# Paired heads in layer B, and a joined, re-laid-out gate and up projection in the experts, of a three-block Trainium2 kernel

## The chip, the core and the metric

The kernel runs on one core of one Trainium2 chip. Its five engines have their own instruction lists: TensorE (PE, matmuls; PEld is its weight load), VectorE (DVE), ScalarE (ACT), GpSimd (POOL) and SyncE (SP, which here only issues DMAs). The metric is device time in microseconds of one execution, lower is better. A change is given against the median of the runs of the kernel before.

## The reference

Three residual blocks work on 512 tokens of 1024 channels, one sequence. The first two are a mixer and a mixture of 16 experts each: block 0 has a dilated attention (layer A here), block 1 the attention with forget gates (layer B). The third is a state-space and pooling block, which the change does not touch. What the change concerns:

```python
def forgetting_mixer(h, w_in, f_bias, w_out, q_gain, k_gain):        # the mixer of layer B
    """logit[t,s] = q_t.k_s/sqrt(d) + sum_{s<j<=t} log sigmoid(w_f.x_j + b_f), causal."""
    ...
    cum = jnp.cumsum(log_f, axis=1).transpose(0, 2, 1)
    q = rmsnorm(qkv[:, :, 0], q_gain) * ATTN_SCALE                   # 16 heads of 64
    k = rmsnorm(qkv[:, :, 1], k_gain)
    ...
    def block(args):                                                 # blocks of 128 queries
        i, q_i, c_i = args
        logits = jnp.einsum('bqhd,bkhd->bhqk', q_i, k).astype(jnp.float32)
        logits = logits + (c_i[..., None] - cum[:, :, None, :])
        mask = key_pos[None, :] <= q_pos[:, None]
        p = jax.nn.softmax(jnp.where(mask, logits, NEG_INF), axis=-1)
        return jnp.einsum('bhqk,bkhd->bqhd', p, v)
    ...
    return o.reshape(b, s, B_WIDTH).astype(h.dtype) @ w_out

def hierarchical_moe(h, wg_r, bg_r, we_r, be_r, w_gate, w_up, w_down):
    """Top-1 expert group, then top-2 experts inside it; SwiGLU experts, weighted by the gate."""
    ...
    gates = (g_onehot[:, :, None] * in_group[:, None, :]).reshape(-1, N_EXPERTS)
    hid = jax.nn.silu(jnp.einsum('nd,edf->nef', t, w_gate)) * jnp.einsum('nd,edf->nef', t, w_up)
    y = jnp.einsum('nef,efd->nd', hid * gates[..., None].astype(hid.dtype), w_down)
    return y.reshape(b, s, d)
```

An expert has a hidden width of 256, so its gate and up weights are 1024 x 256 each, its down weights 256 x 1024.

## The kernel before

One program does everything in sequence: layer A's mixer (0 to some 675 us), its output projection and routing (to 722), the experts of layer 1 (to 922), layer B's start (to 1000), its attention (to 1240), output projection and routing (to 1296), the experts of layer 2 (to 1505), block 2.

*Precision.* A product of two fp32 operands is made of three matmuls over fp32r halves: high times high, high times low, low times high. `split3` (L150, the matmul at L153) issues them. Splitting a weight tile takes an ACT copy to the high half (L315) and a DVE subtraction for the low half (L316). Some operands are left whole ("plain") and go in one fp32 matmul.

*Layer B's attention.* `mix_b` weaves two streams. The background stream is the projection of q, k and v of the head pair that comes later, 24 times three matmuls of 384 columns a pair. The foreground tasks are generators for each head pair: `forget_rows_of` makes normed and transposed q and k (two heads of 64 channels lie on the two halves of the 128 partitions), and `attn_forget`, once for each of the two heads, runs the query blocks 0 to 3. A block's scores have 128, 256, 384 or 512 columns; three matmuls over 64 rows make them in one of three PSUM score tiles (`sc`), and a fourth, of bf16 constants over 128 rows (L1385), adds the causal mask of the diagonal block. `softmax_piece` then takes the bias and the running bound on DVE (L473) and the exponential with its sum on ACT (L474); DVE normalises. `attn_values` transposes the probabilities, splits them, and multiplies by v. `weave` sets the order in which instructions are written: each task yields an estimate of its cost and a delay after which it is due (the numbers in the table `DL`, `bs` and `bp` among them); whichever is due goes in between projections. On PE this order is kept.

*The experts.* Weights are streamed from DRAM by SP. `expert_loads` issues six tiles of 512 KB an expert: gate in two halves, up in two halves, down in two. A tile of gate or up holds four chunks of 128 rows; partition p gets row p of each chunk, so a contiguous piece is one row of 256 numbers, 1 KB. There are 7 staging buffers `est`, 2 of `esp` and 4 extra; `expert_split` frees one when the split is done, and `load(n)` alternates a split and the next load. `token_list` turns an expert's routing ranks into a list of up to 96 tokens (four matmuls of one-hot columns, L949), from which POOL gathers the token rows `xg` from DRAM (`hd`, the normed rows) by an indirect DMA; four more matmuls make the gates (L957). `expert_in` transposes the gathered rows; for the first expert it gives a plain `xTf`, copied by ACT (L1010). `expert_half` runs 24 matmuls of 256 columns over the 8 chunks, once for gate and once for up. `expert_hidden`, `expert_out` and the scatter follow.

*Start of an expert stage.* Routing counts the tokens of each expert. If one has more than 96, an overflow loop has to run; `overflow` reads that flag into a register on every engine, and every engine compares and branches (L1070, L1071). Written order before: list 0, counts, gates, two loads, list 1, two loads, the transposes of the first expert's tokens, the overflow branch, two loads, list 2, loads, gates of experts 0 to 2, then the experts one by one. The data of this case never takes the overflow path.

*Normed rows.* `mix_end` writes the normed rows of each 128 tokens to DRAM after the last scaling (L1194, four a layer).

## Time and profile before

| what | value |
|---|---|
| median of 3 runs | 1851.56 us (1849.99 to 1854.08) |
| profiled execution | 1848.67 us, span of its instructions 1846.8 us |
| mean granted TensorE clock | 0.954 |
| busy, PE / PEld | 1665.7 us (90%) / 1469.2 us (80%) |
| busy, DVE / ACT / POOL | 1282.6 us (69%) / 926.5 us (50%) / 121.0 us (7%) |
| DMA over the whole span | 294141 packets, 310.83 MB, mean 168 GB/s |
| layer B's attention, 1000 to 1240 us | PE 233.55 us, DMA engines 0.20 busy |
| experts of layer 1, 722 to 922 us | PE 174.04 us, DMA engines 0.87 busy, 262 GB/s |
| experts of layer 2, 1296 to 1505 us | PE 173.25 us, DMA engines 0.85 busy, 256 GB/s |

The span runs from the first to the last instruction; the execution's own time is 1.9 us longer. A busy share over the whole span is an average over stages with different limits, so it is read stage by stage. In a timeline, the bracket behind a row is how long the engine had been idle and what ended that. "PEq" is PE's own sequencer: a time in which PE neither computes nor waits for another engine. In the rows, `x8` is eight instructions put together, and the start is that of the first.

### The profile page before, as it was taken

What the parts mean: (1) busy time and instruction counts of PE and PEld (TensorE: products, weight loads), DVE (VectorE), ACT (ScalarE), POOL (GpSimd) and SP (SyncE); (2) the same over time, 40 slices, a digit from 0 to 9 for tenths busy, and PEclk for the clock granted to TensorE, in tenths of its full rate; (3) what the DMA queues carried; (4) which work ended last, traced back from release to release, by engine and by line L of the source; (5) the groups of instructions that cost most, each with busy time, mean ns of one, the idle gap of its engine ahead of it and who ended that gap; (6) DMA issues with size and microseconds to landing.
All of it is one profiled execution on the core that took longest, in us unless ns stands there. A gap on an engine that the chain in (4) does not pass through costs nothing. (4 is left out here: it accounts for less than half of the span.)

```text
span 1846.8 us, 30370 instructions
## 1 busy us (share of the span) xinstructions
PE 1665.7 (90%) x11022; PEld 1469.2 (80%) x11023; DVE 1282.6 (69%) x3181; ACT 926.5 (50%) x1978; POOL 121.0 (7%) x95
## 2 busy tenths in 40 slices
PE   5979999999999996999869999999598959999998
PEld 3878998989989985787658798888487748788886
DVE  6748777767686657787656667666687755998574
ACT  4536556555565643566444555552465533454443
POOL 1000000000000001133200000000133210000000
PEclk9989999999999997999988899899799979999999
DMA  8886655556564136899753221126699953333331
GB/s 291 244 276 183 189 159 176 164 154 195 153 184 132 58 113 211 270 316 302 208 148 93 58 69 58 63 70 212 197 315 313 295 154 110 98 105 88 112 118 76
DMA packets 294141, 310.83 MB, mean 168 GB/s; under 512 B 31263, under 2 KB 240779, under 8 KB 293980
## 3 DMA queue, kind: packets, MB, share of 16 engines
...
## 5 line engine op out<-in xcount | busy, mean ns | idle before, releaser
L153 PE MATMUL mm<-whi,hThi 128*128 128x384 f32 (+2 forms) x1128 | 403.3, 358 | 5.4 <-ACT hThi L739 2.0
L153 PE MATMUL mm<-whi,hTlo 128*128 128x384 f32 (+2 forms) x1128 | 384.3, 341 | 1.0 <-DVE hTlo L740 0.5
L153 PE MATMUL mm<-wlo,hThi 128*128 128x384 f32 (+2 forms) x1128 | 382.6, 339 | 0.0
L316 DVE TENSOR_TENSOR wlo<-wst,whi 128x768 fp32r<-128x768 f32 (+2 forms) x200 | 200.1, 1011 | 67.5 <-ACT whi L315 65.0
L153 PEld LDWEIGHTS mm<-whi,hThi 128*128 128x128 f32 x1128 | 215.6, 191 | 13.9 <-ACT hThi L739 3.2
L315 ACT ACTIVATE whi<-wst 128x768 fp32r<-128x768 f32 (+2 forms) x200 | 176.6, 892 | 87.6 <-PE mm L153 54.2
L153 PEld LDWEIGHTS mm<-whi,hTlo 128*128 128x128 f32 x1128 | 214.9, 191 | 6.2 <-DVE hTlo L740 3.3
L316 DVE TENSOR_TENSOR ehl<-est,ehl 128x1024 fp32r<-128x1024 f32 x144 | 175.8, 1222 | 60.8 <-ACT ehl L315 60.1
L153 PEld LDWEIGHTS mm<-wlo,hThi 128*128 128x128 f32 x1128 | 216.0, 191 | 1.9 <-issue 0.6
L315 ACT ACTIVATE ehl<-est 128x1024 fp32r<-128x1024 f32 x144 | 152.1, 1058 | 105.0 <-PE sc L153 23.3
L153 PE MATMUL mm<-ehl,xTh 128*96 128x256 f32 x960 | 178.4, 287 | 0.0
L248 DVE SCALAR_TENSOR_TENSOR adacc<-ast,csil,adacc 128x512 f32<-128x512 f32 x168 | 126.1, 751 | 64.9 <-DMA ast<-in_w_ada_dram 62.9
L153 PE MATMUL mm<-ehl,xTl 128*96 128x256 f32 x480 | 136.0, 283 | 0.0
L153 PEld LDWEIGHTS mm<-ehl,xTh 128*96 128x96 f32 x960 | 134.7, 165 | 0.0
L153 PE MATMUL mm<-hThi,whi 128*128 128x512 f32 (+1 forms) x288 | 107.2, 372 | 0.7 <-ACT sza L1887 0.6
L153 PE MATMUL mm<-hTlo,whi 128*128 128x512 f32 (+1 forms) x288 | 106.0, 368 | 0.5 <-DVE hTlo L310 0.3
L153 PE MATMUL mm<-hThi,wlo 128*128 128x512 f32 (+1 forms) x288 | 105.8, 367 | 0.0
L415 ACT ACTIVATE raw<-mm 128x256 f32<-128x256 f32 x126 | 48.2, 382 | 110.2 <-PE mm L153 109.8
L420 DVE TENSOR_REDUCE qss<-sq 128x4 f32<-128x256 f32 x128 | 53.0, 414 | 63.3 <-ACT sq L417 63.1
L153 PEld LDWEIGHTS mm<-ehl,xTl 128*96 128x96 f32 x480 | 79.0, 165 | 0.0
L1226 POOL MEMSET xg<- 96x1024 f32 x6 | 5.5, 952 | 1066.5 <-PE sc L153 1066.5
L966 POOL DMA_INDIRECT xd<-y,tidx x32 | 66.6, 2083 | 112.8 <-DVE hTl L1048 87.4
...
## 6 DMA issues: line engine op xcount, KB each, us to landing
ast<-in_w_ada_dram SPq DMA_DIRECT2D x192, 256.0 KB
...
```

The source lines that it names most:

```text
L153: self.nc.tensor.matmul(out, lhsT=l, rhs=r, start=n_first and i == 0, stop=n_last and i == nt - 1)
L248: last = nc.vector.scalar_tensor_tensor(acc, st, self.csil[:, k:k + 1], acc, op0=ALU.mult, op1=ALU.add)
L315: nc.scalar.activation(hi, st, AF.Copy)
L316: nc.vector.tensor_sub(lo, st, hi.bitcast(F32))
L415: nc.scalar.activation(raw[:, t].rearrange("p a b -> p (a b)"), p[:, :256], AF.Copy)
L420: nc.vector.tensor_reduce(ss[:, 4 * t:4 * t + 4], sq.rearrange("p (g d) -> p g d", d=HD), axis=AX.X, op=ALU.add)
L966: self.nc.gpsimd.indirect_dma_start(out=dst, out_offset=bass.IndirectOffsetOnAxis(ap=idx, axis=0), in_=src, in_offset=None, bounds_check=S ...
L1226: nc.gpsimd.memset(xg, 0.0)
```

## The change

It has three parts.

*Layer B.* `attn_forget` is split in two. `forget_scores` takes both heads of a pair at once, in three groups: blocks 0 and 1 together in one score tile a head, then block 2, then block 3. Within a group the matmuls of the two heads alternate; the mask is added by two matmuls of 64 rows a head (`idh`, `maskh`, loaded by four small DMAs of POOL when the layer starts). `forget_values` does the values of both heads, as a task of its own when the scores are done. The planner's delays become `bs` 1.5 and `bp` 3.0, and a probability tile has two buffers.

*Experts.* A staging tile now holds gate and up of two chunks: two DMAs of 256 KB fill it. Partition p holds the rows 8p to 8p+7 of a weight matrix, so a contiguous piece is two neighbouring rows, 2 KB; the number of tiles stays six an expert. For the chunks to match, the normed rows are written with their columns permuted in the last scaling of `mix_end`. `expert_part` makes gate and up in one matmul of 512 columns. The gate terms `tg` get the token columns ahead, so that from expert 2 on one list of four matmuls gives tokens and gates. At the stage's start, the order is: list 0, counts, list 1, gates, the overflow branch, four loads, the transposes, two loads, list 2, loads, gates of experts 0 and 1.

*Small buffers.* Six tiles of the merge in layer A go from two buffers to one.

```diff
+DL.update({'bs': 1.5, 'bp': 3.0})
...
-                              ("tg", [P, NT, 16, 3], BF16)):
+                              ("tg", [P, NT, 16, 5], BF16)):
             R[nm] = self.t(pool, shape, dt, "rt_" + nm)
+        self.nc.gpsimd.tensor_copy(R["tg"][:, :, :, 0:2], self.tokv.unsqueeze(2).to_broadcast([P, NT, 16, 2]))
...
+    def token_list(self, pool, rk, idx, q=P, tg=None, gate=None):
...
+            r = self.tokv[:, t] if tg is None else tg[:, t]
+            nc.tensor.matmul(p[:q, 0:r.shape[-1]], lhsT=oh[:, t], rhs=r, start=t == 0, stop=t == NT - 1)
         nc.vector.tensor_scalar(idx, p[:q, 0:1], p[:q, 1:2], 4096.0, op0=ALU.add, op1=ALU.add)
+        if tg is not None:
+            nc.vector.tensor_reduce(gate, p[:q, 2:5], axis=AX.X, op=ALU.add)
...
-            for nm, nk, n in (("w_gate", 4, F), ("w_up", 4, F), ("w_down", 1, D)):
-                for c in range(2):
...
-                        st = self.t(self.ws, [P, nk, n], F32, "esp" if plain else "est", DL["npl"] if plain else DL["nes"])
...
-                    nc.sync.dma_start(st, dram_ap(a[nm], (l * 16 + e) * D * F + c * nk * P * n, [[n, P], [P * n, nk], [1, n]]))
...
+            for c in range(6):
+                plain = c == 5
+                shp = [P, 2, 2, F] if c < 4 else [P, 1, D]
...
+                else:
+                    st = self.t(self.ws, shp, F32, "esp" if plain else "est", DL["npl"] if plain else DL["nes"])
+                i += 1
+                if c < 4:
+                    for q, nm in enumerate(("w_gate", "w_up")):
+                        nc.sync.dma_start(st[:, q].rearrange("p k f -> p (k f)"),
+                                          dram_ap(a[nm], (l * 16 + e) * D * F + c * 2 * F, [[KC * F, P], [1, 2 * F]]))
...
+                self.staged.append((self.W[e], st))
+                yield
     def expert_split(self):
         if self.staged:
             w, st = self.staged.pop(0)
+            pick = (lambda x: [x[:, :, k] for k in range(2)]) if len(w) < 4 else (lambda x: [x[:, 0]])
             if len(w) == 5 or w is self.W[0]:
-                w.append([(st[:, k],) for k in range(st.shape[1])])
+                w.append([(x,) for x in pick(st)])
                 return
...
-            w.append([(hl[:, 0, k], hl[:, 1, k]) for k in range(st.shape[1])])
+            w.append(list(zip(pick(hl[:, 0]), pick(hl[:, 1]))))
...
+    def expert_part(self, p, x, w, ks):
+        w = [y for c in w[:4] for y in c]
+        for k in ks:
             if len(w[k]) == 1:
                 terms = [(x[k], w[k][0])]
             else:
                 wh, wl = w[k]
                 terms = [(x[0][k], wh), (x[0][k], wl), (x[1][k], wh)]
-            self.split3(p[:self.CAP, o:o + 256], terms, k == 0, k == KC - 1)
+            self.split3(p[:self.CAP].rearrange("p (a b) -> p a b", a=2), terms, k == 0, k == KC - 1)
...
-                nc.vector.scalar_tensor_tensor(h, h, r, shrow, op0=ALU.mult, op1=ALU.add)
-                nc.sync.dma_start(hd[ts, :], h)
+                ho = self.t(pn, [P, D], F32, "hn", 3)
+                by = lambda x: x.rearrange("p (q k) -> p k q", k=KC)
+                nc.vector.scalar_tensor_tensor(ho.rearrange("p (k q) -> p k q", k=KC), by(h), r, by(shrow), op0=ALU.mult, op1=ALU.add)
+                nc.sync.dma_start(hd[ts, :], ho)
...
-            def listed(e):
+            def listed(e, both=False):
                 if e < 16:
-                    ohs = self.token_list(pm, R["rk"][:, :, e], idx[:, e:e + 1], self.CAP)
+                    g = dict(tg=R["tg"][:, :, e], gate=gates[:, e:e + 1]) if both else {}
+                    ohs = self.token_list(pm, R["rk"][:, :, e], idx[:, e:e + 1], self.CAP, **g)
                     self.gather(xgs[e % 3], hd, idx[:, e:e + 1])
                     return ohs
             def gated(e, ohs):
-                if e < 16:
-                    self.token_gates(ohs, [R["tg"][:, t, e] for t in range(NT)], gates[:, e:e + 1], self.CAP)
+                self.token_gates(ohs, [R["tg"][:, t, e, 2:5] for t in range(NT)], gates[:, e:e + 1], self.CAP)
...
                 if e < 16:
                     w = self.W[e]
                     p = self.mm()
-                    self.expert_half(p, 0, xs[e], w[0] + w[1])
+                    self.expert_part(p, xs[e], w, range(4))
...
                         xs[e + 1] = self.expert_in(pm, xgs[(e + 1) % 3])
-                    self.expert_half(p, 256, xs.pop(e), w[2] + w[3])
-                    ohs = listed(e + 3)
-                    gated(e + 3, ohs)
+                    self.expert_part(p, xs.pop(e), w, range(4, KC))
+                    listed(e + 3, True)
                     hid = self.expert_hidden(pm, p)
                 if e:
                     w = self.W[e - 1]
...
             ohs = [listed(0)]
             self.route_counts(self.rt, R)
+            ohs.append(listed(1))
             self.route_gates(self.rt, R["lg"], R)
-            load(2)
-            ohs.append(listed(1))
-            load(2)
+            self.overflow(pm, R, hd, l)
+            load(4)
             with self.tc.manual_schedule(engines={mybir.EngineType.PE}):
                 xs[0] = self.expert_in(pm, xgs[0], True)
-            self.overflow(pm, R, hd, l)
             load(2)
-            ohs.append(listed(2))
+            listed(2, True)
             load(self.NHL - 6)
-            for e in range(3):
+            for e in range(2):
...
+    def forget_scores(self, pool, u, hp, before, then):
...
+        while not (u.get("rows") and self.have_cum and (before is None or before["done"])):
             yield 0, 0.5
...
         yield 0, DL["bq"]
...
+        hs = [slice(h * HD, (h + 1) * HD) for h in range(2)]
...
+        blocks = [[], []]
+        for bs in ((0, 1), (2,), (3,)):
+            p = [self.sc(), self.sc()]
...
+            for b in bs:
+                n = (b + 1) * P
+                q = slice(b * P, n)
+                for i, (x, y) in enumerate(((qh, kh), (qh, kl), (ql, kh))):
+                    for h in range(2):
+                        nc.tensor.matmul(p[h][:, o:o + n], lhsT=x[hs[h], q], rhs=y[hs[h], :n], start=i == 0, stop=False)
+                for c in range(2):
+                    for h in range(2):
+                        nc.tensor.matmul(p[h][:, o + b * P:o + n], lhsT=self.idh[hs[h], c], rhs=self.maskh[hs[h], c],
+                                         start=False, stop=c == 1)
...
+            for h in range(2):
+                o = 0
+                for b in bs:
+                    n = (b + 1) * P
+                    e = self.t(pool, [P, n], F32, f"pexp{h}{b}", 2)
+                    self.softmax_piece(p[h][:, o:o + n], bias[h][:, :n], e, z[h][:, b:b + 1], d[h][:, b:b + 1], n)
...
+            yield cost, DL["bs"]
+        then(blocks)
+    def forget_values(self, pool, u, hp, oT, blocks):
...
+        hs = [slice(h * HD, (h + 1) * HD) for h in range(2)]
...
+        yield from self.attn_values(pool, "b", blocks, hs, terms, lambda h, o: nc.scalar.activation(oT[hs[h], hp], o, AF.Copy))
+        u["done"] = 2
...
+            self.idh, self.maskh = [self.t(pq, [P, 2, P], BF16, nm) for nm in ("idh", "maskh")]
+            for out, off in ((self.idh, OFF_ID), (self.maskh, OFF_MASK)):
+                for h in range(2):
+                    nc.gpsimd.dma_start(out[h * HD:(h + 1) * HD],
+                                        dram_ap(self.a["c_tab"], off, [[N_CONST, HD], [HD * N_CONST, 2], [1, P]]))
...
-                    for h in range(2):
-                        fg.append((h, self.attn_forget(pa, u, hp, h, oT), DL["bu"] + h * DL["bo"]))
+                    fg.append(("scores", self.forget_scores(pa, u, hp, hist[hp - 2] if hp > 1 else None, lambda blocks: fg.append(
+                        ("values", self.forget_values(pa, u, hp, oT, blocks), DL["bp"]))), DL["bu"]))
...
```

Three places show what moves. First, PE in layer B's attention, at the scores: `sc` are the score tiles, `kTh`/`kTl` and `qTh`/`qTl` the halves of k and q, and columns stand last. Before, the first three blocks of one head:

```order
L153 MATMUL sc_12868<-kTh_2657_12813,qTh_2648_12785 128x128
L153 MATMUL sc_12868<-kTl_2658_12814,qTh_2648_12785 128x128
L153 MATMUL sc_12868<-kTh_2657_12813,qTl_2649_12786 128x128
L1385 LDWEIGHTS identb_432
L1385 MATMUL sc_12868<-maskb_434,identb_432 128x128
L153 MATMUL sc_12878<-kTh_2657_12813,qTh_2648_12785 128x256
L153 MATMUL sc_12878<-kTl_2658_12814,qTh_2648_12785 128x256
L153 MATMUL sc_12878<-kTh_2657_12813,qTl_2649_12786 128x256
L1385 LDWEIGHTS identb_432
L1385 MATMUL sc_12878<-maskb_434,identb_432 128x128
L153 MATMUL sc_12890<-kTh_2657_12813,qTh_2648_12785 128x384
```

Now, the first group of a pair, blocks 0 and 1 (two score tiles, one for each head):

```order
L1402 MATMUL sc_11928<-kTh_2527_11893,qTh_2524_11878 128x128
L1402 MATMUL sc_11929<-kTh_2527_11893,qTh_2524_11878 128x128
L1402 MATMUL sc_11928<-kTl_2528_11894,qTh_2524_11878 128x128
L1402 MATMUL sc_11929<-kTl_2528_11894,qTh_2524_11878 128x128
L1402 MATMUL sc_11928<-kTh_2527_11893,qTl_2525_11879 128x128
L1402 MATMUL sc_11929<-kTh_2527_11893,qTl_2525_11879 128x128
...
L1405 MATMUL sc_11928<-maskh_11239,idh_11238 128x128
...
L1405 MATMUL sc_11929<-maskh_11239,idh_11238 128x128
L1402 MATMUL sc_11928<-kTh_2527_11893,qTh_2524_11878 128x256
L1402 MATMUL sc_11929<-kTh_2527_11893,qTh_2524_11878 128x256
...
L1405 MATMUL sc_11929<-maskh_11239,idh_11238 128x128
L154 MATMUL mm_11970<-whi_11750,hThi_11229 128x384
```

Each head's terms stood alone, with one mask of 128 rows behind them; now two heads alternate, and four masks of 64 rows stand behind each block's terms.

Second, PE at the start of the first layer's experts: `oh` are one-hot token columns, `tokv` the token numbers, `xg` the gathered rows, `xTf` their transposed copy. Before:

```order
L949 MATMUL tp_8968<-tokv_436,oh_8969 96x2
L1008 MATMUL tp_8986<-cst_63,xg_1814_8911 128x96 x4
L1008 MATMUL tp_8992<-cst_63,xg_1814_8911 128x96 x4
L1070 TENSOR_LOAD rt_anyi_8937
L1071 COMPARE_AND_BRANCH
...
L1071 UNCONDITIONAL_BRANCH
...
L949 MATMUL tp_9451<-tokv_436,oh_9452 96x2
...
L957 MATMUL tp_9477<-rt_tg_8259,oh_8920 96x3
L153 MATMUL mm_9497<-est_8471,xTf_8985 96x256 x3
```

Now:

```order
L952 MATMUL tp_8950<-tokv_432,oh_8951 96x2
L1083 TENSOR_LOAD rt_anyi_8946
L1084 COMPARE_AND_BRANCH
...
L1084 UNCONDITIONAL_BRANCH
L1019 MATMUL tp_9447<-cst_63,xg_1816_8920 128x96 x4
L1019 MATMUL tp_9453<-cst_63,xg_1816_8920 128x96 x4
L952 LDWEIGHTS oh_9465
L952 MATMUL tp_9464<-rt_tg_8255,oh_9465 96x5
...
L154 MATMUL mm_9508<-est_8469,xTf_9446 96x512
```

The branch (L1071 before, L1084 now) stood behind the transposes of `xg` and stands ahead of them; the third token list has five columns, and the first expert matmul 512.

Third, ACT at the same place, where `ehl` is the high half of a weight tile. Before:

```order
L315 ACTIVATE ehl_9560<-x_1781_8750 128x1024
L315 ACTIVATE ehl_9565<-x_1809_8885 128x1024
L1010 ACTIVATE xTf_8985<-tp_8986 128x384
L1010 ACTIVATE xTf_8985<-tp_8992 128x384
L1070 TENSOR_LOAD rt_anyi_8937
L1071 COMPARE_AND_BRANCH
...
L1071 UNCONDITIONAL_BRANCH
L315 ACT_TABLE_LOAD
L315 ACTIVATE ehl_9572<-est_8964 128x1024
L315 ACTIVATE ehl_9577<-est_8966 128x1024
```

Now:

```order
L316 ACTIVATE ehl_9564<-x_1811_8894 128x1024
L316 ACTIVATE ehl_9571<-est_9432 128x1024
L1083 TENSOR_LOAD rt_anyi_8946
L1084 COMPARE_AND_BRANCH
...
L1084 UNCONDITIONAL_BRANCH
L1021 ACT_TABLE_LOAD
L1021 ACTIVATE xTf_9446<-tp_9447 128x384
L316 ACTIVATE ehl_9577<-est_9435 128x1024
L1021 ACTIVATE xTf_9446<-tp_9453 128x384
L316 ACTIVATE ehl_9583<-est_9438 128x1024
```

Both copies to `xTf` stood ahead of the branch and now stand behind it and behind a table load; a split of an `est` tile that stood behind the branch stands ahead of it.

## Rows read from the trace of the kernel before

**Rows 1.** Busy by window: stretch, length, PE, PEld, DVE, ACT, POOL, clock, DMA, GB/s

```profile
1000.00:1240.00 240.00, 233.55 (x1567) 201.89 (x1568) 158.01 (x546) 127.53 (x320) 0.00 (x0) 0.92 0.20 61
752.00:922.00 170.00, 159.69 (x1134) 131.05 (x1134) 127.37 (x190) 94.95 (x147) 47.05 (x27) 0.98 0.93 279
1326.00:1490.00 164.00, 153.92 (x1110) 128.51 (x1111) 125.49 (x186) 92.87 (x142) 45.54 (x26) 0.97 0.94 286
```

**Rows 2.** Chain of waits in the second expert stage: start us, us, what

```profile
1370.78 13.54 DMA est<-in_w_down_dram
```

**Rows 3.** Timeline, all engines, 728.5 to 745 us: start, us, engine, line, what, [idle before]

```profile
729.20 1.51 PE L1008 MATMUL tp<-cst,xg 96*128 96x96 f32 x8 [4.84 <-DMA xg<-hd,tidx]
...
731.62 1.28 ACT L315 ACT_TABLE_LOAD   x1 [0.38 <-ACTq L1071]
...
733.99 1.06 ACT L315 ACTIVATE ehl<-est 128x1024 fp32r<-128x1024 f32 x1 [1.09 <-DMA est<-in_w_gate_dram]
...
736.34 0.45 PE L949 MATMUL tp<-tokv,oh 128*96 128x2 bf16 x4 [5.62 <-PEq L1071]
...
736.97 1.15 PE L153 MATMUL mm<-est,xTf 128*96 128x256 f32 x2
...
742.51 2.23 SPq L988 DMA_DIRECT2D est<-in_w_up_dram  x2
```

**Rows 4.** Timeline of PE in layer B, one head's scores, 1118.5 to 1122.6 us

```profile
1118.95 0.33 PE L153 MATMUL sc<-kTh,qTh 64*128 64x128 f32 x1
...
1119.43 0.23 PE L1385 MATMUL sc<-maskb,identb 128*128 128x128 bf16 x1
1119.59 0.38 PE L153 MATMUL sc<-kTh,qTh 64*128 64x256 f32 x1
...
1122.10 0.42 PE L153 MATMUL mm<-whi,hThi 128*128 128x384 f32 x1
```

**Rows 5.** Timeline of PE in layer A, two heads' scores, 158.0 to 159.6 us

```profile
158.40 0.33 PE L548 MATMUL sc<-kTh,qTh 64*128 64x128 f32 x2
158.56 0.27 PE L548 MATMUL sc<-kTl,qTh 64*128 64x128 f32 x2
158.67 0.27 PE L548 MATMUL sc<-kTh,qTl 64*128 64x128 f32 x2
...
159.28 0.44 PE L153 MATMUL mm<-whi,hThi 128*128 128x384 f32 x1
```

**Rows 6.** Chain of waits: an expert's half of 256 columns; block 2's matmuls of 512

```profile
1418.81 2.82 PE mm L153 x24
...
1798.22 1.36 PE mm L153 x6
```

**Rows 7.** Layer A's score line (L548): what PE waited for, us and times

```profile
  DVE zN L473: 2.7, 6
```

**Rows 8.** Timeline of PE, behind one expert's up half, 1334 to 1346 us

```profile
1334.59 0.32 PE L957 MATMUL tp<-rt_tg,oh 128*96 128x3 bf16 x4
1334.77 1.08 PE L153 MATMUL sc<-est,hTf 128*96 128x512 f32 x2
```

**Rows 9.** DMA from 1370 to 1480 us: all packets; weights' queue (packets, MB, share)

```profile
DMA packets 23283, 32.97 MB, mean 300 GB/s; under 512 B 1836, under 2 KB 19733, under 8 KB 23273
...
q1 hardware_dynamic: 21200, 28.29, 79.0%
```

**Rows 10.** DMA from 28 to 33 us: the queue, and what was issued (KB each)

```profile
q1 hardware_dynamic: 1060, 1.93, 104.9%
...
ast<-in_w_ada_dram SPq DMA_DIRECT2D x8, 256.0 KB
```

**Rows 11.** Two lines of VectorE: duration in ns, shortest/median/longest, and shapes

```profile
L1194 DVE SCALAR_TENSOR_TENSOR hn<-hn,tn_r,rh x8: 1274/1277/1283, 691.8 to 1291.7; 128x1024 f32<-128x1024 f32 x8
...
L461 DVE SCALAR_TENSOR_TENSOR qTl<-tp,gqk,qTh x16: 712/954/1178, 73.2 to 1213.8; 128x512 fp32r<-128x512 f32 x16
```

**Rows 12.** Layer B's softmax piece on VectorE (L473): duration in ns, shortest/median/longest

```profile
L473 DVE CUSTOM_DVE_ANT_0 pexp<-sc,biasF x64: 273/489/692, 1000.7 to 1223.9; 128x128 f32<-128x128 f32 x16, 128x256 f32<-128x256 f32 x16, 128x384 f32<-128x384 f32 x16, 128x512 f32<-128x512 f32 x16
```

83 lines of the change are left out of this document (31 added, 52 removed).

## The prediction

> **What bounds the kernel now.** I read the page's busy times first: TensorE (PE) is by far the busiest engine, so the sum goes by stages, and I ask in each whether PE works or waits. The busy time by windows gives that [rows 1]. In layer B's attention (1000 to 1240 us) PE is busy for 233.55 of 240 us and the DMA engines for 0.20 of them: only fewer PE microseconds shorten it. In the two expert stages PE is idle for 10.3 of 170 us and 10.1 of 164 us, while the DMA engines stand at 0.93 and 0.94: both limits are close together there. The chain of waits says which ends last: in the second expert stage it runs for 13.54 us at a stretch through arriving down weights [rows 2], the first of four such stretches between 1370 and 1470. So weights pace the middle of the stage, PE its rest. At the stage's start, after routing, the timeline of all engines shows a hole in which PE does almost nothing from 724 to 737 us [rows 3]. The change touches these three places.
>
> **Layer B, paired heads.** Before, one head's four query blocks are 12 score matmuls and 4 masks; they start at 1118.95 and the next projection starts at 1122.10, 3.15 us [rows 4], or 6.30 us for two heads. The same pairing already runs in layer A: there two heads' terms of 128 and 256 columns (six rows of two instructions) take 158.40 to 159.28 = 0.88 us [rows 5], whereas in layer B one head alone needs 0.48 us for its three terms of 128 columns (1118.95 to 1119.43 [rows 4]). So two matmuls on the two halves of the rows go side by side. For the blocks of 384 and 512 columns I take one unpaired step for both heads: 0.23 us for 512 columns (1.36 us for six [rows 6]) and three quarters of it, 0.17, for 384; three each, 1.2 us. The masks become 16 matmuls over 64 rows instead of 8 over 128. No row shows one. Not under 0.06 us each (half of the 0.11 us step of two 128-column matmuls in layer A's list, 1.0 us a pair of heads), not over the 0.16 us that one takes now (1119.43 to 1119.59 [rows 4], 2.6 us); I take 0.09, 1.5 us, nearer to the paired rows. A pair then costs 0.88 + 1.2 + 1.5 = 3.6 us (3.1 to 4.7), and eight pairs save 8 x (6.3 - 3.6) = 21.6 us (12.8 to 25.6).
>
> Against that: a pair of heads takes two of three score tiles, so each of the 24 groups waits until VectorE has read the group before. In layer A, 16 such groups (64 matmuls of each term, four a group) waited 2.7 us in all [rows 7], 0.17 us each, or 4 us for 24. Twelve projection matmuls (12 x 0.17 = 2.1 us) stand between two groups of a pair, and the order has VectorE's reads of all a group's tiles ahead of its normalising, so a tile is free about 1.7 us after the group. At a few spots, late in the stage, the order has no projections left between a head's transposes and its values, so that PE waits there for the copies of ScalarE and VectorE; I price this at another 1 us (0 to 4). **Layer B gains 21.6 - 5 = 17 us (9 to 24)**. The second probability buffer, the planner's new delays and the mask's loads by GpSimd cost nothing, as DMA is at 0.20 in that stage; without that cover the four small loads would be a few microseconds once.
>
> **Experts, joined gate and up.** An expert's 48 matmuls of 256 columns run in two halves, 24 in 2.82 us [rows 6], 118 ns each. They become 24 of 512 columns; six of these take 1.36 us [rows 6], 227 ns each. 48 x 0.118 - 24 x 0.227 = 0.21 us. The four gate matmuls that followed each token list (0.16 us [rows 8]) are folded into the list's own for experts 2 to 15. Together 0.37 us an expert, 14 experts, 5.2 us of PE a layer, worth something only where PE, not DMA, is late.
>
> **Experts, rows of 2 KB.** In the middle of the stage the weights' queue moves 21200 packets, 28.29 MB, in 79.0% of 16 engines' 110 us [rows 9]: 65.6 ns a packet of 1.33 KB, 20.3 GB/s an engine. Gate and up come as 1 KB rows; after the change two neighbouring rows come as one of 2 KB. A stretch of 2 KB rows is in the trace: 28 to 33 us, the adaptive weights, 1060 packets, 1.93 MB at 104.9%: 79 ns, 23.0 GB/s an engine, 1.93 MB / 5 us = 386 against 300 GB/s in all [rows 9, 10]. By the engines' rate the 2.1 MB of an expert's gate and up fall from 6.4 to 5.7 us (-0.7), by the whole rate from 7.0 to 5.4 (-1.6); the software queue of gathers and scatters, 18.5%, is in the second. Over 14 experts DMA would need 10 to 22 us less. PE can only use its idle 10.3 us and the 5.2 us above, 15.5 at most. I take 11, near the lower DMA bound, since that one is PE's idle too. Twice as many DMAs of half the size do not weigh against it in this trace: the fast stretch was made of 256 KB DMAs [rows 10], the new size.
>
> The Trainium skill speaks against it (DMA: Bandwidth & Descriptors, Bandwidth): batch DMAs to 1 MiB or more. The 386 GB/s of 256 KB DMAs disagree; by the rule this term would be at or below nothing.
>
> **Start of the expert stage.** Before, PE waits 4.84 us for the first gather, transposes, and then is held 5.62 us by the branch over the overflow code [rows 3]. The new order puts the branch right behind the second token list, into the gather's wait. PE alone would then transpose at about 731 to 733. But xTf, its input for the first expert, is copied by ScalarE, and ScalarE's order now has a sixth weight split ahead of its branch. That split's DMA is issued at the same place, and the split can't start before 733.99 [rows 3]; plus 1.06 us, 0.4 us of branch and the table load of 1.28 us, which now stands ahead of the copy, the first copy starts at about 736.7 and the first expert matmul at 737.2, against 736.97. So I cost the move at nothing for PE (bounds: 0.5 us late, 6 us early). Late next is ScalarE. VectorE's gates for two experts now stand behind one matmul instead of sixteen, so its next splits come some 2 us earlier, and with them SP's next loads (742.51 before [rows 3]); with DMA pacing the stage that is worth 0 to 3 us, I take 1. Queued behind the waiting branch are SP's loads, but four are issued ahead of it.
>
> **Permuted normed rows.** The last step writes its 1024 columns in another order: 1.28 us now, four a layer, the fourth on the chain to routing. A strided output cost VectorE 1178 against 712 ns at 512 columns (longest and shortest in [rows 11]); so 1.28 becomes up to 2.1 us: -0.8 us a layer (0 to -2). Merge buffers from two to one: nothing, VectorE runs its list in order; the bound is a wait of the 0.2 us kind, eight times.
>
> **Sum.** 17 + 2 x (11 + 1 - 0.8) = 39 us from the profiled 1848.67 us: 1809. The runs' median, 1851.56, is 2.9 above that execution, so the same sum from it is 1812. I predict **1810**, between them.
>
> **Rivals.**
> 1. *Rows of 2 KB are not quicker here* (0.17). For it: the fast stretch has no gathers beside it, and 4 KB rows already make a third of the bytes. Then arriving weights still pace the stage, PE's 5.2 us vanish into waits, some 3 us a layer remain: 17 + 6 = 23, 1827 by the same middle. The Trainium skill's 512 B as the least transfer for full rate (same page, Specifications) would have it so; 300 against 386 GB/s speaks against it.
> 2. *The moved branch is really hidden* (0.10). If ScalarE's split lands early, the first expert begins 5 us sooner in both layers: 1800. Against it: the landing at 733.99.
> 3. *Score tiles run out* (0.06), the slower side. If VectorE doesn't read ahead, and each group waits for both heads' softmax in series (the max alone is 0.49 us at the median [rows 12]; with the exponential, its sum, the reciprocal and the scaling behind it, an estimate of four times that, 2 us a head; 4 less the 2.1 us of projections), 24 x 1.9 = 46 us against 21.6: layer B loses 24, and with 22 from the experts the time is 1853. It decides from 1.7 us a group. Layer A's 0.17 us speaks against it.
> 4. *The pairs do not run side by side in layer B* (0.07), as masks between the terms change what is loaded: no gain there, the experts' 22 remain: 1829.
>
> **How the numbers follow.** My forecast has 0.60; its own range is 1800 to 1822 (layer B 9 to 24, experts 8 to 14 a layer). The range 1794 to 1837 takes in rivals 1, 2 and 4 and leaves out the third and the tails. A difference under 0.2% (3.7 us) can't be told from none. Faster 0.89, same 0.04, slower 0.07: rival 3 with a rest for mechanisms that I don't see.
>
> **What would show it.** In layer B: score groups of two heads in 0.9 to 1.3 us, waits of PE on the max's result below 5 us, the stage some 17 us shorter. In the experts: weights' packets about half in number at 23 GB/s an engine, stretches of arriving weights in the chain gone or halved, PE idle under 5 us. At the start: PE's first expert matmul within 1 us of before, held by ScalarE's copy; if it comes 5 us sooner, that step was wrong. If layer B keeps its 240 us, the pairing was; if PE still idles 10 us, the rows were.

## The result, and the profile after

The kernel after takes 1822.84 us (median of 4 runs, 1819.79 to 1824.57) against 1852.39 us for the kernel before (4 runs). The ratio is 0.984 with a 95% interval of 0.9822 to 0.9858: 29.5 us faster, where 41.6 us were predicted (1851.56 to 1810). The profiled execution took 1824.57 us, its span is 1822.6 us and the mean granted clock 0.961 (before 0.954). The total lies inside the predicted range; the terms behind it do not all lie inside theirs.

The page's first part, engine by engine (busy us, share of the span, instructions), and its DMA line:

```profile
PE 1624.6 (89%) x10222; PEld 1381.7 (76%) x10223; DVE 1285.6 (71%) x3181; ACT 919.7 (50%) x1975; POOL 123.9 (7%) x101
...
DMA packets 263995, 310.90 MB, mean 171 GB/s; under 512 B 33887, under 2 KB 177867, under 8 KB 263836
```

PE lost 41 us of busy time, while the profiled execution is only 24 us shorter (1848.67 to 1824.57): PE now waits more. The bytes are the same in 30,000 fewer packets.

The busy time by windows answers to [rows 1]: layer B from its first to its last score mask, then the middle of the two expert stages. For layer B the first fence has the same stretch, first to last mask, of the kernel before.

```profile
999.00:1223.00 224.00, 217.55 (x1440) 186.83 (x1439) 150.75 (x530) 120.15 (x307) 0.00 (x0) 0.93 0.20 59
```

And of the kernel after:

```profile
1003.00:1203.00 200.00, 183.78 (x1508) 166.03 (x1506) 147.58 (x527) 114.20 (x305) 0.00 (x0) 0.97 0.23 67
757.00:920.00 163.00, 150.92 (x710) 98.23 (x710) 125.30 (x186) 94.03 (x144) 46.67 (x27) 0.97 0.93 292
1297.00:1463.00 166.00, 152.61 (x721) 99.00 (x720) 127.70 (x191) 95.38 (x146) 44.50 (x27) 0.98 0.94 295
```

In the expert windows PE is still idle for 12.1 of 163 us and 13.4 of 166 us, with the DMA engines at 0.93 and 0.94 as before. In layer B PE's idle time went from 6.45 to 16.2 us.

To see what each edit did, I divide every trace at the same instructions. "Layer B" runs from the first to the last mask, "route" from the first product of the normed rows to the first one-hot list on VectorE, "start" from that list to the first expert matmul, "experts" from there to the last hidden product; all in us.

| kernel | route 1 | start 1 | experts 1 | layer B | route 2 | start 2 | experts 2 |
|---|---|---|---|---|---|---|---|
| before | 44.7 | 14.4 | 178.4 | 224.5 | 53.6 | 14.9 | 177.6 |
| after | 51.4 | 15.0 | 172.7 | 199.3 | 53.5 | 15.3 | 171.4 |
| pair_only | 44.7 | 14.0 | 182.3 | 199.8 | 50.7 | 14.5 | 176.8 |
| rows_1kb | 44.7 | 14.2 | 181.2 | 199.2 | 51.1 | 15.0 | 175.2 |
| hn_plain | 44.7 | 14.5 | 171.4 | 199.1 | 51.0 | 15.2 | 168.5 |
| hold_split | 50.8 | 11.1 | 173.9 | 198.9 | 53.9 | 11.1 | 171.2 |
| own_buffer | 46.0 | 15.0 | 170.8 | 199.4 | 51.6 | 15.9 | 172.3 |
| one_behind_other | 50.7 | 15.0 | 171.4 | 202.0 | 53.5 | 15.2 | 167.9 |
| no_scatter | 49.8 | 14.6 | 157.7 | 199.1 | 53.9 | 15.6 | 156.1 |
| plain_and_hold | 44.7 | 11.1 | 174.2 | 199.4 | 50.5 | 11.1 | 171.0 |
| after_again | 50.5 | 14.7 | 169.1 | 199.4 | 53.6 | 14.9 | 170.1 |
| by_head | 50.3 | 14.8 | 170.1 | 221.4 | 53.5 | 15.5 | 169.5 |
| hn_plain_again | 44.7 | 14.5 | 170.8 | 199.7 | 50.5 | 15.5 | 170.3 |
| plain_hold_again | 44.7 | 11.1 | 176.2 | 199.2 | 51.0 | 11.1 | 171.3 |

Route, start and layer B repeat within 1.5 us where the code is the same; the experts scatter by up to 4 us (178.4 and 182.3 in before and pair_only, 172.7 and 169.1 in after and after_again). Layer A is not in the table: the first product of route 1 falls at 677.9 us in before and at 683.1 in pair_only, with the same code ahead of it, and anywhere from 676.5 to 683.8 us in the others. That scatter hides whatever the smaller merge buffers cost, and a single profile's total is worth less than its stages.

### The profile page after: what moved, and what is told of

Same layout as the page of the kernel before. It is cut to its first block, busy times and chain, and to the rows that moved or that the text cites. A ratio compares the mean times of both kernels' runs of the same rounds, so it can differ in the third digit from the quotient of the medians.

```text
span 1822.6 us, 29089 instructions
## 1 busy us (share of the span) xinstructions
PE 1624.6 (89%) x10222; PEld 1381.7 (76%) x10223; DVE 1285.6 (71%) x3181; ACT 919.7 (50%) x1975; POOL 123.9 (7%) x101
## 3 DMA queue, kind: packets, MB, share of 16 engines
q1 hardware_dynamic: 255708, 291.89, 51.1%
## 5 line engine op out<-in xcount | busy, mean ns | idle before, releaser
L317 DVE TENSOR_TENSOR ehl<-est,ehl 128x1024 fp32r<-128x1024 f32 x144 | 175.7, 1220 | 61.5 <-ACT ehl L316 47.2
L154 PE MATMUL mm<-ehl,xTh 128*96 128x512 f32 x480 | 153.3, 400 | 0.0
L154 PE MATMUL mm<-ehl,xTl 128*96 128x512 f32 x240 | 94.8, 395 | 0.0
L154 PEld LDWEIGHTS mm<-ehl,xTh 128*96 128x96 f32 x480 | 73.2, 162 | 25.8
L489 DVE TENSOR_TENSOR pTl<-tp,pTh 128x512 fp32r<-128x512 f32 (+1 forms) x112 | 68.4, 628 | 23.3 <-ACT pTh L488 22.6
L154 PE MATMUL av<-pTh,vhi 128*64 128x128 f32 x400 | 77.7, 230 | 0.4 <-ACT pTh L488 0.4
L487 PE MATMUL tp<-cst,pexp 128*128 128x128 f32 x400 | 64.2, 279 | 15.4 <-DVE pTl L489 11.7
```

What stands on the lines that cost most here:

```text
L154: self.nc.tensor.matmul(out, lhsT=l, rhs=r, start=n_first and i == 0, stop=n_last and i == nt - 1)
L317: nc.vector.tensor_sub(lo, st, hi.bitcast(F32))
L487: nc.tensor.transpose(p[:, j * q:(j + 1) * q], blocks[c + j], self.ident[:q, :q])
L489: self.mark = nc.vector.tensor_sub(lo[:, :m * q], p[:, :m * q], hi[:, :m * q].bitcast(F32))
```

## The experiments

Each was timed against the kernel before on the same chip. There are three chips: one with pair_only, hn_plain, rows_1kb and hold_split (before 1853.58 us), a second with own_buffer, one_behind_other, no_scatter and plain_and_hold (1846.06), a third with the other four (1849.53). Absolute times compare only within a chip, so across chips I use ratios.

**pair_only**: the kernel before with layer B's part alone (pairing, masks of 64 rows, the planner's delays, the second probability buffer).

```diff
-fg.append((h, self.attn_forget(pa, u, hp, h, oT), DL["bu"] + h * DL["bo"]))
+fg.append(("scores", self.forget_scores(pa, u, hp, ...), DL["bu"]))
 # experts, normed rows, merge buffers: as before
```

> The kernel before with the paired heads of layer B alone. Theory: between first and last score of layer B the changed kernel is 24.8 us shorter than the kernel before, made of some 21 us of matmuls side by side, some 14 us from a granted clock that no longer halves while one head's scores run alone, and 10 us given back to new waits on the copies of the probabilities. If that stage stands for itself, this kernel takes 1825 to 1831 us (22 to 27 less than before), and no stretch at 0.50 follows a run of scores. Rival: the stage's gain needs the rest of the change (other stages' loads, other order) and this kernel gains 17 us or less, with half-clock stretches left in layer B.

Measured: 1829.94 us (1825.04 to 1834.33), ratio 0.9871 [0.985, 0.9892], 23.6 us faster; layer B takes 199.8 us, as in the kernel after. Layer B's part alone gives four fifths of the whole gain.

**by_head**: the kernel after, each score group split by head, with one score tile and a break for the planner behind each head.

```diff
-            p = [self.sc(), self.sc()]
-            ... both heads' matmuls, alternating ...
+            for h in range(2):
+                p = self.sc()
+                ... one head's matmuls ...
+                yield cost, DL["bs"] / 2
```

> The changed kernel with the score groups split by head: each of the three groups of a pair becomes two, one head each, with some six projection matmuls between them, so that matmuls on the two halves of the rows can no longer run at the same time (when only the order inside a group was turned, the second head's matmuls still started beside the first's, 1100.83 and 1100.84 us, and the stage grew by 2.7 us only). Masks, buffers and number of matmuls stay. Theory: side by side is the larger part: a pair's scores take 3.2 us now and took 6.3 at full clock; 8 x 3 = 24 us more, the stage at 215 to 225 us, the time 16 to 26 us above the changed kernel; the clock stays up, since short runs of scores alternate with projections. Rival: the clock was the larger part (14 us of half-clock time in the kernel before); then the stage stays below 210 us as long as no 0.50 stretch follows the scores, and the time within 10 us.

Measured: 1839.84 us (1832.43 to 1848.05), ratio 0.9953 [0.9931, 0.9975], against 1817.67 for after_again on the same chip: +22.2 us. Layer B takes 221.4 us, +22.0. That is what two heads side by side are worth, net of waits: PE is idle for 13.4 us of the stage here, for 16.2 in the kernel after. The rest of layer B's part is worth little by itself, 3.1 us in the stage (224.5 to 221.4). PE's timeline (start, us, engine, line, what) shows that the two heads' first matmuls of a group now stand 2.4 us apart, projections between them:

```profile
1104.62 0.32 PE L1402 MATMUL sc<-kTh,qTh 64*128 64x128 f32 x1
...
1105.77 0.44 PE L154 MATMUL mm<-whi,hThi 128*128 128x384 f32 x1
...
1107.02 0.32 PE L1402 MATMUL sc<-kTh,qTh 64*128 64x128 f32 x1
```

**one_behind_other**: the kernel after, within a group all of head 0's terms and masks, then all of head 1's, with nothing between.

```diff
-                for i, (x, y) in enumerate(((qh, kh), (qh, kl), (ql, kh))):
-                    for h in range(2):
+                for h in range(2):
+                    for i, (x, y) in enumerate(((qh, kh), (qh, kl), (ql, kh))):
```

> The changed kernel with another order inside a group of scores: first all terms and masks of the first head (upper half of the rows), then all of the second head, instead of in turns. Everything else is the same. Theory: what layer B gained is that two heads' matmuls run side by side and that the granted clock stays up; with the heads one behind the other a group takes nearly twice as long (24 groups x 0.8 us or more) and stretches at 0.50 come back behind the score groups, so the stage between first and last score goes from 199 us to 218 or more and the time to 1840 to 1858. Rival: the gain is from fewer switches between scores and projections and the masks' new form; then the stage stays within 8 us of 199 and the time below 1832.

Measured: 1822.7 us, ratio 0.9892 [0.9859, 0.9926]; layer B 202.0 us, only 2.7 longer than after's. I had thought that this order undoes the pairing; for the most part it does not. In PE's timeline the third row, by its place head 1's first matmul, starts 0.01 us behind head 0's second one, three matmuls ahead of where the program writes it:

```profile
1100.55 0.44 PE L1402 MATMUL sc<-kTh,qTh 64*128 64x384 f32 x1
1100.83 0.33 PE L1402 MATMUL sc<-kTl,qTh 64*128 64x384 f32 x1
1100.84 0.44 PE L1402 MATMUL sc<-kTh,qTh 64*128 64x384 f32 x1
...
1101.68 0.45 PE L154 MATMUL mm<-whi,hThi 128*128 128x384 f32 x1
```

The profile models the end of a matmul, so I go from start to start: this group of two heads with its masks takes 1.13 us, while in by_head one head's group of 384 columns alone takes 0.85 (1109.40 to 1110.25). In the kernel after, where the heads alternate, the two together take that same 0.85 (1138.08 to 1138.93). So most of the overlap needs no alternating order, and the order is worth the rest, 0.3 us here. What moved the third row forward, the engine or the compiled order, no view of this kernel shows. The Trainium skill (TensorEngine Tiling (Array Packing), Key Properties) says that different tiles of the array can run matmuls in parallel; the trace agrees. The ratio is higher than after's by 0.5%, more than 2.7 us explain; it comes from another chip, and this stays open.

**rows_1kb**: the kernel after with plain normed rows, and weights again as rows of 1 KB (gate and up joined, the branch moved, the list folded).

```diff
-nc.sync.dma_start(st[:, q].rearrange("p k f -> p (k f)"), dram_ap(a[nm], ... + c * 2 * F, [[KC * F, P], [1, 2 * F]]))
+nc.sync.dma_start(st[:, q], dram_ap(a[nm], ... + c * 2 * P * F, [[F, P], [P * F, 2], [1, F]]))
```

> As the kernel with plain normed rows, but the weights of gate and up come in rows of 1 KB, by chunks of 128 rows as in the kernel before (still two DMAs of 256 KB a tile, gate and up joined). Theory: the expert stages' DMA engines move 310 to 314 GB/s with 1 KB rows and with 2 KB rows alike, so the larger rows bring nothing: within 3 us of the plain kernel with 2 KB rows, and if that is at 1817, 1815 to 1820. Rival, the step of the prediction: 2 KB rows are quicker by 0.7 to 1.6 us an expert; then this one is 10 us or more slower than the plain kernel with 2 KB rows, at 1827 or more.

Measured: 1821.03 us (1814.07 to 1829.81), ratio 0.9819 [0.9794, 0.9844]. The weights' queue from 1340 to 1440 us (packets, MB, share of 16 engines):

```profile
q1 hardware_dynamic: 20669, 26.49, 82.3%
```

26.49 MB in 82.3% of 16 engines' 100 us is 20.1 GB/s an engine, the old rate. The time lies between the two that I had set against each other (no gain from 2 KB rows, or 10 us and more). This kernel's profiled execution, 1829.81 us, is its slowest, 8.8 us above the median, so its stages in the table are on the long side.

**hn_plain** and **hn_plain_again** (one kernel on two chips): the kernel after, with normed rows in their plain order. The transposes pick every eighth column instead, so weights stay at 2 KB a row.

```diff
-                ho = self.t(pn, [P, D], F32, "hn", 3)
-                nc.vector.scalar_tensor_tensor(ho.rearrange("p (k q) -> p k q", k=KC), by(h), r, by(shrow), ...)
-                nc.sync.dma_start(hd[ts, :], ho)
+                nc.vector.scalar_tensor_tensor(h, h, r, shrow, op0=ALU.mult, op1=ALU.add)
+                nc.sync.dma_start(hd[ts, :], h)
...
-    xg[:, k * P:(k + 1) * P]
+    xg.rearrange("p (q k) -> p k q", k=KC)[:, k]
```

> The changed kernel, but the normed rows are written in their own order again and the transposes of the gathered rows read every eighth column instead; the weights' 2 KB rows stay. Theory: the permuted write (2.0 to 2.3 us instead of 1.28) lengthens routing by 6.7 us in the first layer and by nothing in the second, so this kernel is 4 to 8 us faster than the changed one, 1815 to 1819 us. Rival: strided reads cost TensorE as much in 32 sets of transposes (0.66 us each now) as they save, or the first layer's delay is taken back by weights that then arrive later: within 2 us of the changed kernel, 1821 to 1825.

> The kernel with plain normed rows and strided transposes once more, on one chip with the changed kernel. Theory: 6 to 10 us below it (8.8 across two chips; 6.5 and 2.7 us by the length of routing in the two layers). Rival: some of that was the chip, and it is 5 us or less.

Measured: 1814.09 us (1811.82 to 1816.03), ratio 0.979 [0.9771, 0.9808], and 1812.18 us (1807.53 to 1814.19), 0.9795 [0.9762, 0.9828], against 1817.67 for after_again beside it. Route 1 is back at 44.7 us. Its weights' queue moves 27.50 MB in 79.7% of the engines' time from 1330 to 1430 us, 21.6 GB/s an engine. From rows_1kb to hn_plain it is 6.9 us, but with ranges that overlap.

**own_buffer**: the kernel after, with the permuted rows in a buffer name of their own.

```diff
-                ho = self.t(pn, [P, D], F32, "hn", 3)
+                ho = self.t(pn, [P, D], F32, "ho", 2)
```

> The changed kernel, with one edit: the permuted normed rows go to two buffers of their own instead of sharing three with the unscaled rows. Plain rows (the kernel before this one) gave back 8.8 us: routing took 44.7 and 51.0 us instead of 51.4 and 53.5. Theory A: most of it is the buffer, since two tiles a step then share three, and the next step's first product is put behind the long scaling; then this kernel has routing at 46 to 48 and 51 to 52 us and takes 1815 to 1819. Theory B: it is the longer instruction itself (2.0 to 2.3 us against 1.28, four a layer); then routing stays at 50 us or more in the first layer and the time within 2 us of the changed kernel's 1822.8.

Measured: 1815.67 us, ratio 0.9833 [0.981, 0.9855]; route 46.0 and 51.6 us. The scaling on VectorE (duration in ns, shortest/median/longest) in this kernel:

```profile
L1209 DVE SCALAR_TENSOR_TENSOR ho<-hn,tn_r,rh x8: 2050/2193/2233, 693.4 to 1259.9; 128x1024 f32<-128x1024 f32 x8
```

On this chip one_behind_other, which has the shared buffer, takes 7.0 us more (1818.26 to 1829.92 against 1811.6 to 1816.04); its other order of scores is 2.6 of them by layer B's stage.

**hold_split**: the kernel after, with the sixth to eighth weight splits (ScalarE's copy and VectorE's subtraction) issued behind ScalarE's copy of the first expert's tokens.

```diff
+            if 6 <= self.nsp <= 8:
+                with self.tc.issue_after(self.xtf.ins):
+                    self.split_weights(hl[:, 0], hl[:, 1], st)
```

> The changed kernel with one edit: from the sixth weight split on, ScalarE and VectorE do the first splits only behind the copies of the first expert's transposed rows. Theory: ScalarE's sixth split, which waits for a DMA until 743.2, is what keeps the moved branch from saving anything; without it the first expert matmul comes at 740 to 743 rather than at 746.6 (VectorE's own branch, 740.9, is late next), and the time falls by 3 to 8 us to 1815 to 1820. Rival: the start moves up but arriving weights pace the stage, so the expert stage ends when it did: within 2 us of the changed kernel.

Measured: 1821.06 us (1817.68 to 1821.93), ratio 0.9826 [0.9807, 0.9845]. Both starts are 11.1 us, 4 shorter, so the split ahead of ScalarE's copy was what held PE there. The time falls by less than 2 us against the kernel after, as in the rival of the expectation.

**plain_and_hold** and **plain_hold_again** (one kernel): hn_plain and hold_split together.

> The kernel with plain normed rows (1814.1) and the held splits together. Held splits alone brought the first expert matmul 4 us forward in both layers, and the time from 1822.8 to 1821.1. Theory: arriving weights pace the stage, and of 8 us some 2 remain: 1810 to 1815. Rival: with routing shorter, the start is what counts, and the gain is the whole 8 us: 1804 to 1808.

> Plain normed rows and held splits once more, on one chip with the kernel without the hold. The first expert matmul comes 4 us earlier in each layer, but the experts then take 2.5 to 2.8 us longer, by the profiles. Theory: arriving weights pace the stage, and 1 to 4 us in all remain. Rival: the earlier start is kept, 6 to 8 us.

Measured: 1808.75 us, ratio 0.9805 [0.9781, 0.983], and 1810.41 us (1804.27 to 1820.43), 0.9794 [0.9755, 0.9832]. On the third chip its median is 7.3 us below the kernel after's, with ranges that overlap; from hn_plain_again it cannot be told (1.8 us less, ranges overlapping). The hold shortens the start (plain_hold_again):

```profile
737.46 1.51 PE L1024 MATMUL tp<-cst,xg 96*128 96x96 f32 x8 [7.55 <-DVEq L1089]
...
738.37 1.13 ACT L1026 ACTIVATE xTf<-tp 128x384 f32<-128x384 f32 x2 [4.95 <-PE tp L1024]
...
739.25 2.00 PE L154 MATMUL mm<-est,xTf 128*96 128x512 f32 x2
```

but the experts that follow are 174.2 and 176.2 us long in layer 1 against 171.4 and 170.8 without it.

**no_scatter**: the kernel after without the scatter-adds, and without the gathers from the fourth expert on; it reads what the gathers have left.

```diff
-        self.scatter(R["xd"], idx, y)
...
-                    self.gather(xgs[e % 3], hd, idx[:, e:e + 1])
+                    if e < 3:
+                        self.gather(xgs[e % 3], hd, idx[:, e:e + 1])
```

> The changed kernel without the scatter-adds of all experts' outputs and without the gathers from the fourth expert on (so the experts add nothing to the result). In the expert stages the DMA engines move 310 to 315 GB/s, whether gate and up come in rows of 1 KB or of 2 KB, and the software queue of these gathers and scatters takes 19 to 20% of the engines' time for 14% of the bytes. Theory: the engines are full, and what the weights lack is that queue's time: then weights move at 340 GB/s or more in 100 us of the stage, TensorE stops waiting, and an expert stage is 8 us or more shorter. Rival: weights are bound elsewhere (memory, or the number of loads in flight): the weights' queue stays at 27 MB in 100 us and the stage's length within 4 us.

Measured: 1783.23 us (one run). The experts shrink to 157.7 and 156.1 us. Busy by window, a stretch of 100 us in layer 1's experts of this kernel:

```profile
780.00:880.00 100.00, 99.06 (x496) 66.05 (x494) 91.87 (x137) 70.17 (x104) 0.00 (x0) 1.00 0.91 309
```

and of the kernel after:

```profile
790.00:890.00 100.00, 88.80 (x431) 58.22 (x430) 79.20 (x120) 60.24 (x91) 30.09 (x18) 0.97 0.98 310
```

Without the software queue the bound changes sides: PE is busy for 99.06 of 100 us and the DMA engines fall from 0.98 to 0.91. All queues together stay at 309 GB/s and do not reach the 340 that I had put down, since PE is now the bound. The weights' queue alone carries what all queues carried:

```profile
q1 hardware_dynamic: 14173, 30.82, 90.6%
```

**after_again**: the kernel after, on the third chip.

> The changed kernel once more, as the base for the others of this call on one chip. All theories: 1.4 to 1.8% under the kernel before, routing of the first layer at 50 to 52 us, first to last score of layer B in 199 us.

Measured: 1817.67 us (1814.34 to 1826.32), ratio 0.9846 [0.9809, 0.9882]; the result repeats.

## Why the prediction was right or wrong, point by point

The gain by steps, from medians on one chip: pairing -23.6 us (before to pair_only), joining, branch and folded list -8.9 (to rows_1kb), rows of 2 KB -6.9 (to hn_plain, with its strided transposes), and permuted rows +5.5 (hn_plain_again to after_again, the third chip) to +8.8 (the medians of hn_plain and of the kernel after, which were not timed together). Together -31 to -34, against -29.5 and -31.9 measured.

That the total fell inside the range is partly luck: layer B gave 25 us where 17 were forecast, in part by a clock that no step had, and made up for some of what the experts (22 forecast, 15.8 timed for joining and rows) and the permuted rows lacked.

**Layer B: the mechanism right, the sum too small.** Predicted 21.6 for the pairing and 5 of new waits, 17 in all (9 to 24); measured 25.2 us in the stage (224.5 to 199.3), above the range, and 23.6 by pair_only's time. Side by side is worth 22.0 by by_head, so the 21.6 was close. PE's timeline of a group of two heads (512 columns and masks) answers to [rows 4]:

```profile
1141.22 0.50 PE L1402 MATMUL sc<-kTh,qTh 64*128 64x512 f32 x2
1141.56 0.40 PE L1402 MATMUL sc<-kTl,qTh 64*128 64x512 f32 x2
1141.79 0.39 PE L1402 MATMUL sc<-kTh,qTl 64*128 64x512 f32 x2
1142.03 0.29 PE L1405 MATMUL sc<-maskh,idh 64*128 64x128 bf16 x4
1142.24 0.45 PE L154 MATMUL mm<-whi,hThi 128*128 128x384 f32 x1
```

Two heads' 512 columns take 0.81 us for three terms, where I took 0.69; four masks of 64 rows take 0.21 us, 0.05 each, where I took 0.09 and not under 0.06. The two errors partly cancel: where nothing interrupts them, the three groups of a pair take 1.15, 0.85 and 1.02 us (from the trace, start to start), 3.0 us where 3.6 was taken and 6.3 before.

The waits were not 5 but some 10 us more. What PE waited for in layer B (us, times, longest):

```profile
PE tp L487 <- DVE pTl L489: 11.7, 7, 5.4
PE tp L448 <- DVE pTl L489: 2.5, 2, 1.8
PE sc L1402 <- DVE fzz L474: 0.7, 2, 0.5
```

The score tiles, for which 4 us were priced, cost 0.7; the third rival has no ground, and by by_head the fourth has none either. The copies behind the transposes, priced at 1 us (0 to 4), cost 14.2 (2.8 before), the longest 5.4, late in the stage (PE is busy for 2.93 of the 8 us from 1179). They do not come from the paired scores: by_head, with its scores apart, has nearly the same ones:

```profile
PE tp L487 <- DVE pTl L489: 10.3, 7, 5.4
PE tp L448 <- DVE pTl L489: 2.5, 2, 1.8
```

That the values of both heads now come in one run with no projection left to put between is argued from the order, not tried.

What paid for that is the clock, which no step had. Before, PE's granted clock fell from 1.00 to 0.50 (2.4 to 1.2 GHz) in four stretches of layer B. One of them by windows of 4 us, where the last columns are clock, DMA share and GB/s:

```profile
1044.00:1048.00 4.00, 4.00 (x45) 3.55 (x43) 1.51 (x5) 2.12 (x6) 0.00 (x0) 1.00 0.01 2
1048.00:1052.00 4.00, 4.00 (x16) 2.63 (x15) 2.80 (x12) 2.32 (x8) 0.00 (x0) 0.73 0.03 12
1052.00:1056.00 4.00, 4.00 (x12) 2.57 (x11) 2.12 (x11) 1.72 (x6) 0.00 (x0) 0.50 0.20 55
1056.00:1060.00 4.00, 4.00 (x14) 3.76 (x14) 2.11 (x7) 0.90 (x3) 0.00 (x0) 0.50 0.19 66
1060.00:1064.00 4.00, 4.00 (x29) 3.65 (x28) 2.22 (x5) 2.19 (x6) 0.00 (x0) 0.99 0.00 0
```

PE did not pause in these 20 us; up to the fall it had run the twelve score matmuls and four masks of one head (1046.62 to 1049.77), the twelve on half of the rows, without a projection between. The other stretches are 1001 to 1012, 1182 to 1193 and 1220 to 1228 us, each at the end of such a run or within one. In the kernel after the clock falls only where PE had waited: the windows with 0.79 are those from 1027, 1123 and 1187 us, each behind or around a wait of 1.1 to 5.4 us. Over the stage the mean clock went from 0.93 to 0.97: 0.07 x 224 = 15.7 us against 0.03 x 200 = 6.0, some 10 us given back, an estimate that takes PE's time to go with its clock and, with a clock of two digits, is good to some 2 us. By the same reckoning PE's own work at full clock fell by 24 us (217.55 - 15.7 = 201.9 against 183.78 - 6.0 = 177.8), the clock gave 10 and the idle time took 10. by_head's clock is 0.98 though its heads stand alone, six projections apart; so it is the long run of one head's scores that the fall goes with in the trace of before, not the single heads, and the spacing by the new delays has a share in this gain, not the pairing alone. Why it fell in four places only, of eight pairs of heads, is open.

**Experts: the mechanism right, the size too large.** Predicted 11 us a layer (8 to 14). Of all traces, those with 1 KB rows (before, pair_only, rows_1kb) have 180.6 and 176.5 us on average for the two layers, those with 2 KB rows and no hold (without no_scatter) 170.9 and 170.0: 9.7 and 6.5, or 8 a layer. That holds joining as well as rows, and it is rather too large: the profiled executions of pair_only and rows_1kb lie 3.7 and 8.8 us above their medians. By the timed medians the 2 KB rows give 6.9 us for both layers. By the prediction's own sign, PE still idle for 10 us (12.1 and 13.4 here), the rows were the wrong step. The step that failed is "DMA would need 10 to 22 us less", worked out from 23.0 GB/s an engine and 386 GB/s in all, both of a stretch of 5 us [rows 10]. The weights' queue from 780 to 880 us in the kernel before and from 790 to 890 us in the kernel after:

```profile
q1 hardware_dynamic: 20305, 26.52, 80.9%
...
q1 hardware_dynamic: 12059, 26.41, 78.6%
```

And the kernel after in layer 2, 1335 to 1435 us:

```profile
DMA packets 14269, 31.52 MB, mean 315 GB/s; under 512 B 2236, under 2 KB 2236, under 8 KB 14261
...
q1 hardware_dynamic: 12259, 26.80, 78.6%
...
q0 software_dynamic: 2002, 4.62, 19.9%
```

26.80 MB in 78.6% is 21.3 GB/s an engine, against 20.2 before (26.16 MB in 80.8% of 1360 to 1460 us): +5% in layer 2. In layer 1 it is 21.0 against 20.5, +2.5%. 13% was taken. The packets did fall by 40%. The Trainium skill (DMA: Bandwidth & Descriptors, Why small descriptors are slow) gives a fixed overhead of about 3 cycles a packet beside 32 bytes a cycle; two rows of 1 KB are 70 cycles and one of 2 KB is 67, an estimate of 4% on gate and up, or of 3% on the whole stream, a third of which has rows of 4 KB before and after. The traces' 2.5 and 5% are of that order. no_scatter has 21.3 as well (30.82 MB in 90.6%), so it is not the gathers and scatters that lower an engine's rate on weights; 23.0 does not come back in any of these stretches of 100 us. What the software queue takes is time: 19.9% of it for 15% of the bytes. Without it the weights run at 30.8 MB per 100 us instead of 26.4 in layer 1, 31.0 instead of 26.8 in layer 2, and PE becomes the bound. The chain of waits still has a stretch of arriving weights, 10.27 us where [rows 2] had 13.54:

```profile
1350.78 10.27 DMA est<-in_w_down_dram
```

Rival 1 is half right: the rows are quicker, but by less than half of what was taken. What joining and folding alone give is not settled: the timing says 8.9 us (pair_only to rows_1kb), the experts' stages of the two profiles 2.7 (359.1 to 356.4), though rows_1kb's profile lies 5.1 us further above its median than pair_only's. The four folded gate matmuls take 0.18 us from start to start before [rows 8], where the prediction read 0.16: 0.3 us more a layer.

**Start: right.** The first expert matmul comes 0.4 to 0.6 us later than before against the list, at the late bound of 0.5, and it is ScalarE that holds it. The timeline of all engines answers to [rows 3]:

```profile
741.01 1.51 PE L1019 MATMUL tp<-cst,xg 96*128 96x96 f32 x8 [7.55 <-DVEq L1084]
...
743.21 1.06 ACT L316 ACTIVATE ehl<-est 128x1024 fp32r<-128x1024 f32 x1 [7.70 <-DMA est<-in_w_up_dram]
...
744.45 1.28 ACT L1021 ACT_TABLE_LOAD   x1 [0.18 <-ACTq L1084]
745.75 0.49 ACT L1021 ACTIVATE xTf<-tp 128x384 f32<-128x384 f32 x1
...
746.63 1.15 PE L154 MATMUL mm<-est,xTf 128*96 128x512 f32 x1
```

The split waits for its load, then branch, table load, copy: the predicted order, and rival 2 falls with it. PE transposes 9.3 us behind the list's 731.67, where 8.4 to 10.4 was expected (731 to 733 against 722.6 before). SP's next loads do come earlier, 13.9 us behind the list (745.55) where they came 19.9 behind it (742.51 [rows 3]); whether that gave the 1 us priced for it no run separates. And the hold shows why a better start is worth little: it wins 8 us in the two starts and 1.8 us of time, by hn_plain_again and plain_hold_again, which can't be told from none. The experts behind it are longer by 4 us in layer 1 and by 2 in layer 2: weights pace the stage (in hn_plain arriving weights are 86% of the chain of waits from 1325 to 1435 us), and PE catches up with them sooner.

**Permuted normed rows: the step that failed most.** Predicted -0.8 us a layer (0 to -2). The routing of layer 1 went from 44.7 to 51.4 us, that of layer 2 stayed at 53.5, but pair_only and hn_plain have 50.7 and 51.0 there: 6.7 and 2.7, some 9 us, and 5.5 us timed on one chip. The scaling's own price was near, up to 2.1 us taken [rows 11]; after:

```profile
L1209 DVE SCALAR_TENSOR_TENSOR hn<-hn,tn_r,rh x8: 2041/2273/2320, 693.9 to 1271.0; 128x1024 f32<-128x1024 f32 x8
```

+1.0 us for the last of four. The rest is the buffer. `ho` takes a second of the three "hn" tiles in each of the four steps, and VectorE's order has to put the next products behind the scaling that frees one. In own_buffer the instruction is as slow (2193 ns) but the routing takes 46.0 and 51.6 us: 5.4 of the 6.7 us and 1.9 of the 2.7 are the shared buffer. VectorE's first products and first scaling in the kernel after:

```profile
680.24 0.55 DVE L1195 TENSOR_TENSOR hn<-x,rs 128x384 f32<-128x384 f32 x1
...
684.71 0.56 DVE L1195 TENSOR_TENSOR hn<-x,rs 128x384 f32<-128x384 f32 x1
...
691.24 0.42 DVE L1195 TENSOR_TENSOR hn<-x,rs 128x256 f32<-128x256 f32 x1
...
693.90 2.32 DVE L1209 SCALAR_TENSOR_TENSOR hn<-hn,tn_r,rh 128x1024 f32<-128x1024 f32 x1
696.21 0.54 DVE L1195 TENSOR_TENSOR hn<-x,rs 128x384 f32<-128x384 f32 x1
```

and in own_buffer:

```profile
679.50 0.55 DVE L1195 TENSOR_TENSOR hn<-x,rs 128x384 f32<-128x384 f32 x1
...
680.44 0.55 DVE L1195 TENSOR_TENSOR hn<-x,rs 128x384 f32<-128x384 f32 x1
...
681.49 0.56 DVE L1195 TENSOR_TENSOR hn<-x,rs 128x384 f32<-128x384 f32 x1
...
683.97 0.56 DVE L1195 TENSOR_TENSOR hn<-x,rs 128x384 f32<-128x384 f32 x1
...
690.50 0.42 DVE L1195 TENSOR_TENSOR hn<-x,rs 128x256 f32<-128x256 f32 x1
```

Four products of 384 columns stand ahead of the first one of 256 where two stand in the kernel after, and there the next product starts at 696.21, right when the scaling ends. Own_buffer's ratio, 0.9833 against 0.984 and 0.9846 on other chips, does not show the 7 us by itself; on its own chip it is 7.0 us below one_behind_other, of which some 4 are left for the buffer when that kernel's order of scores is taken off. The prediction looked at the instruction's length and not at whose buffer it took, though the diff names "hn". Why route 2 got 3 us shorter by the pairing alone is open.
